# Both MLP products of a transformer block as seven block products instead of eight

## The chip, the core and the metric

The kernel runs on one core of one Trainium2 chip. The core has five engines that run side by side, each with an in-order queue of its own: TensorE (PE, the 128x128 multiplier; PEld is its loading of the stationary operand), VectorE (DVE), ScalarE (ACT), GpSimd (POOL) and SyncE (SP). SP, ACT and POOL also issue transfers, which 16 DMA engines carry out. SBUF is the memory on the chip, PSUM the accumulators of TensorE, DRAM the memory behind the DMA engines. The metric is the time of one execution in microseconds, the median of several.

## The reference, cut to what matters

One layer of a streaming encoder over 512 tokens of width 2048: attention first, then a squared-ReLU MLP of width 8192, both residual, and a final norm.

```
def sq_relu_mlp(h, w1, w2):
    return jnp.square(jax.nn.relu(h @ w1)) @ w2
...
    h = h + stick_breaking_mixer(rms_norm(h, norm_mix), w_qkv, w_o)
    h = h + sq_relu_mlp(rms_norm(h, norm_mlp), w1, w2)     # w1 2048 x 8192, w2 8192 x 2048
    return rms_norm(h, final_norm)                          # 512 x 2048
```

Everything is float32. A product is exact to about float32 by splitting each operand into two float32r parts, hi and lo, and adding three products: hi hi, hi lo, lo hi.

## The kernel before

A *panel* is 512 columns of a weight matrix against all 512 tokens. Its weights come in *pieces* of two contraction tiles (256 rows, 512 KB): `load` issues the transfer into `raw` on SP, `split` makes `whi` (ACT, L142) and `wlo = raw - whi` (DVE, L143), and `run` multiplies. `mm3` (L149) issues the three products of one tile pair on lines 151 to 153, each with its own load of the stationary operand. Pieces go round in six buffers of `wp` (three pieces of two parts) and two of `rp`.

The program runs 12 panels for q, k and v with the attention's steps woven in, four panels of the output projection (`o_panels`; `turn_h` transposes the new residual stream into `hT` on TensorE and splits it), and then the MLP: eight chunks of 1024 hidden columns, each two panels of W1 (16 contraction tiles; `evac_1` makes relu, square and the split of it in SBUF) and four panels of W2 (8 contraction tiles; `evac_2` adds the product, times the token's scale, to the residual tiles `hn`). The last W2 panel is computed token block by token block (`run_held`, accumulators `acch`), its last block in two halves of 256 columns, so that the final norm (`finish`) overlaps. In the MLP the residual stream `hn` (16 tiles) and the activations stay in SBUF.

The order on each engine is that of the code as the tile framework's scheduler placed it when the program was built; each engine then works through its own list and waits on semaphores where another engine's result is missing.

Of the kernel before, what the change touches and what calls it, by code (L numbers as in the profile page):

```python
# [12 lines left out]
PSUM = bass.MemoryType.PSUM  # L13

# [11 lines left out]
FC = 1024            # hidden columns of the MLP held on chip at a time  # L26


class Panel:
    """512 weight columns against all 512 tokens: four accumulators of one PSUM bank."""  # L30

    def __init__(self, srcs, nk, acts, weights_still, evac, held=False):
        self.held = held                    # all its weights are on chip at once
# [8 lines left out]
def trunk_kernel(  # L42
    ctx: ExitStack,
    tc: tile.TileContext,
    x: bass.AP,          # [512, 2048], last token first
    x_t: bass.AP,        # its transpose
    g_mix: bass.AP,      # [128, 16]
    g_mlp: bass.AP,      # [128, 16]
    g_fin: bass.AP,      # [1, 2048]
# [4 lines left out]
    out: bass.AP,        # [512, 2048], last token first  # L54
# [6 lines left out]
    acc_a = ctx.enter_context(tc.tile_pool(name="acc_a", bufs=4, space=PSUM))  # L61

# [6 lines left out]
    # ---- constants  # L69
# [15 lines left out]
    ss_h, ms_h, rstd2 = stat[:, 20:36], stat[:, 36:40], stat[:, 40:44]  # L85
# [4 lines left out]
    def rsqrt(dst, v, t0, t1):  # L90
        """dst = v ** -0.5, with one Newton step after the table's square root."""
# [7 lines left out]
    # ---- weight pieces: raw by DMA, then an exact split into two float32r parts  # L99
# [28 lines left out]
    def split(n):  # L128
        while state["split"] < min(n, len(pieces)):
            i = state["split"]  # L130
            load(i + 1)
            raw = raws.pop(i)
            if pieces[i][0].held:
                parts = [(slot(F32R, "whi"), slot(F32R, "wlo")) for _ in range(G)]
                for j, (hi, lo) in enumerate(parts):
                    nc.scalar.copy(hi, raw[:, j, :])
                    nc.vector.tensor_tensor(out=lo, in0=raw[:, j, :], in1=f(hi), op=ALU.subtract)
            else:
                hi = wp.tile([P, G, W], F32R, name="whi", tag="w")
                lo = wp.tile([P, G, W], F32R, name="wlo", tag="w")  # L140
                for js in halves(i):
                    nc.scalar.copy(hi[:, js, :], raw[:, js, :])  # L142
                    nc.vector.tensor_tensor(  # L143
                        out=lo[:, js, :], in0=raw[:, js, :], in1=f(hi[:, js, :]), op=ALU.subtract)
                parts = [(hi[:, j, :], lo[:, j, :]) for j in range(G)]
            splits[i] = parts
            state["split"] += 1

    def mm3(ps, a, b, start, stop):  # L149
        """ps += a.T @ b for (hi, lo) pairs."""  # L150
        nc.tensor.matmul(ps, lhsT=a[0], rhs=b[0], start=start, stop=False)  # L151
        nc.tensor.matmul(ps, lhsT=a[0], rhs=b[1], start=False, stop=False)  # L152
        nc.tensor.matmul(ps, lhsT=a[1], rhs=b[0], start=False, stop=stop)  # L153
# [6 lines left out]
    def run(p, pool, step=None, steps=1, before_held=False):  # L160
        banks = [pool.tile([P, W], F32, name=f"acc{b}", tag="acc") for b in range(4)]
        ng = p.nk // G
        for g in range(ng):
            i = p.first_piece + g
            ahead(i)
            if before_held and g >= 2:
                ahead(i + 1)
# [19 lines left out]
    def run_held(p, pool, spans):  # L187
        """Token block by token block; spans[b] are the column ranges of its accumulators."""
        split(len(pieces))
        parts = [q for g in range(p.nk // G) for q in splits.pop(p.first_piece + g)]  # L190
        for b in range(4):
            ca = slice(b * P, (b + 1) * P)
            for cs in spans[b]:
                bank = pool.tile([P, W], F32, name="acch", tag="acc")
                for k in range(p.nk):
                    act = p.acts(k)
                    hi, lo = parts[k]
                    mm3(bank[:, 0 : cs.stop - cs.start], (act[0][:, ca], act[1][:, ca]), (hi[:, cs], lo[:, cs]),
                        k == 0, k == p.nk - 1)
                p.evac(b, bank, cs)  # L200

    # ---- the attention's panels
    xT, oT, hT = {}, {}, {}
    qT, kT, vv = {}, {}, {}

    def evac_v(grp):
# [333 lines left out]
```

## Time and profile before

| | |
|---|---|
| median of 3 runs | 2197.77 us (2197.66 to 2198.48) |
| span of the profiled execution, first to last instruction | 2196.5 us |
| TensorE busy | 2184.8 us, 99% |
| VectorE busy | 869.6 us, 40% |
| ScalarE busy | 666.0 us, 30% |
| GpSimd busy | 36.8 us, 2% |
| moved by DMA | 216.53 MB, 99 GB/s |

The page gives the span of the profiled execution, 2196.5 us, 1.3 us below the median of the runs (2197.77), which also holds what lies before the first and behind the last instruction; a time that is summed from the trace is made against the span, and those 1.3 us are added. Matmuls overlap in the array, so their rate is read from the distance between the starts of neighbours, not from the length of one.

### The profile page before, as it was taken

Reading aid. Unit: us, or ns where it says so; the run is one execution under the profiler, and the core shown is the slowest. Engines: PE = TensorE matmul, PEld = TensorE weight load, DVE = VectorE, ACT = ScalarE, POOL = GpSimd, SP = SyncE. Lnnn points to the kernel's source line nnn. Section 1 sums busy time; section 2 is a strip of 40 time slices with the busy share of each in tenths; the row PEclk is TensorE's granted clock in tenths of the full one; section 3 lists DMA queues with packets and bytes.
Section 4 is the critical chain, followed back from the end, with each engine's and each line's share of the span. In section 5 each row is a group of like instructions: output and inputs, shape, how many; then the busy total and the mean of one; then the engine's idle time right before and its main releaser. Section 6 shows DMA issues by size and latency. Waiting matters only on the chain.

```text
span 2196.5 us, 23826 instructions
## 1 busy us (share of the span) xinstructions
PE 2184.8 (99%) x9870; PEld 1812.8 (83%) x9870; DVE 869.6 (40%) x1024; ACT 666.0 (30%) x897; POOL 36.8 (2%) x91
## 2 busy tenths in 40 slices
PE   9999999999999999999999999999999999999998
PEld 7888888888888888888888888888888888888887
DVE  7354453553553333433333333333332433343334
ACT  6343342442442332212212212212211311221234
POOL 0000000000010000000000000000000000000013
PEclk9999999999999999999999999999999999999999
DMA  5222222222234333333233333333323333333323
GB/s 192 96 77 81 92 77 87 85 79 95 79 115 134 106 96 96 96 96 96 97 98 99 100 96 96 96 96 96 96 97 97 99 99 98 96 96 96 96 96 125
DMA packets 129101, 216.53 MB, mean 99 GB/s; under 512 B 8016, under 2 KB 40800, under 8 KB 128864
## 3 DMA queue, kind: packets, MB, share of 16 engines
q1 hardware_dynamic: 125360, 207.66, 30.7%
q10 hardware_dynamic: 3600, 7.34, 1.0%
q8 instruction: 77, 1.26, 0.2%
q14 instruction: 32, 0.26, 0.0%
q0 software_dynamic: 32, 0.01, 0.0%
HBM read 210.78 MB, written 4.19 MB: 98 GB/s over the span
## 4 chain that ended last, share of the span: by engine, by line
PE 98%; DMA 1%; DVE 0%; ACT 0%; issue 0%; SPq 0%; ACTq 0%
PE acc L151 31%; PE acc L153 31%; PE acc L152 31%; PE at L443 1%; DMA raw<-w_qkv_dram 0%; PE z L152 0%; PE ot L152 0%; PE z L153 0%; PE ot L153 0%; PE z L151 0%; PE ot L151 0%; PE acch L153 0%; PE acch L152 0%; PE acch L151 0%; PE at L258 0%; DMA xc<-x_t_dram 0%
## 5 line engine op out<-in xcount | busy, mean ns | idle before, releaser
L143 DVE TENSOR_TENSOR wlo<-raw,whi 128x1024 fp32r<-128x1024 f32 (+1 forms) x381 | 466.8, 1226 | 1080.9 <-ACT whi L142 1077.1
L142 ACT CAST whi<-raw 128x1024 fp32r<-128x1024 f32 (+1 forms) x381 | 400.4, 1051 | 1235.0 <-PE acc L152 1221.0
L151 PE MATMUL acc<-thi,whi 128*128 128x512 f32 x1536 | 599.8, 390 | 0.0
L153 PE MATMUL acc<-thi,wlo 128*128 128x512 f32 x1536 | 598.1, 389 | 0.0
L152 PE MATMUL acc<-tlo,whi 128*128 128x512 f32 x1536 | 597.7, 389 | 0.0
L151 PE MATMUL acc<-whi,ahi 128*128 128x512 f32 x992 | 385.9, 389 | 0.0
L152 PE MATMUL acc<-wlo,ahi 128*128 128x512 f32 x992 | 385.9, 389 | 0.0
L153 PE MATMUL acc<-whi,alo 128*128 128x512 f32 x992 | 385.9, 389 | 0.0
L153 PEld LDWEIGHTS acc<-thi,wlo 128*128 128x128 f32 x1536 | 288.3, 188 | 60.5
L152 PEld LDWEIGHTS acc<-tlo,whi 128*128 128x128 f32 x1536 | 288.4, 188 | 58.9
L151 PEld LDWEIGHTS acc<-thi,whi 128*128 128x128 f32 x1536 | 288.4, 188 | 59.0
L152 PEld LDWEIGHTS acc<-wlo,ahi 128*128 128x128 f32 x992 | 186.2, 188 | 38.7
L153 PEld LDWEIGHTS acc<-whi,alo 128*128 128x128 f32 x992 | 186.2, 188 | 38.7
L151 PEld LDWEIGHTS acc<-whi,ahi 128*128 128x128 f32 x992 | 186.2, 188 | 38.6
L151 PE MATMUL acc<-whi,ohi 128*128 128x512 f32 x256 | 101.2, 395 | 0.0
L152 PE MATMUL acc<-wlo,thi 128*128 128x512 f32 x256 | 100.1, 391 | 0.6 <-DVE wlo L143 0.6
L151 PE MATMUL acc<-whi,thi 128*128 128x512 f32 x256 | 100.3, 397 | 0.5 <-ACT whi L142 0.5
L153 PE MATMUL acc<-whi,olo 128*128 128x512 f32 x256 | 100.0, 390 | 0.0
L153 PE MATMUL acc<-whi,tlo 128*128 128x512 f32 x256 | 99.9, 391 | 0.0
L152 PE MATMUL acc<-wlo,ohi 128*128 128x512 f32 x256 | 99.7, 389 | 0.0
L284 DVE SCALAR_TENSOR_TENSOR h<-acc,stat,h 128x512 f32<-128x512 f32 x112 | 83.2, 749 | 34.1 <-PE acc L153 34.1
L432 DVE TENSOR_TENSOR_SCAN rest<-rest,first 128x512 f32<-128x512 f32 (+1 forms) x64 | 52.5, 820 | 15.6 <-ACT rest L430 15.6
(109 smaller groups left out, 1238.4 us busy)
## 6 DMA issues: line engine op xcount, KB each, us to landing
raw<-w_dram SPq DMA_DIRECT2D x256, 512.0 KB, 3.7
raw<-w_qkv_dram SPq DMA_DIRECT2D x130, 256.0 KB, 3.0
raw<-w_o_dram SPq DMA_DIRECT2D x32, 512.0 KB, 3.6
raw<-w_qkv_dram SPq DMA_DIRECT2D x31, 512.0 KB, 3.8
h<-x_dram ACTq DMA_DIRECT2D x16, 256.0 KB, 4.0
xc<-x_t_dram SPq DMA_DIRECT2D x7, 512.0 KB, 4.9
y_dram<-h SPq DMA_DIRECT2D x8, 256.0 KB, 3.3
y_dram<-h ACTq DMA_DIRECT2D x8, 256.0 KB, 3.4
```

Source lines behind the costliest of these rows:

```text
L142: nc.scalar.copy(hi[:, js, :], raw[:, js, :])
L143: nc.vector.tensor_tensor(out=lo[:, js, :], in0=raw[:, js, :], in1=f(hi[:, js, :]), op=ALU.subtract)
L151: nc.tensor.matmul(ps, lhsT=a[0], rhs=b[0], start=start, stop=False)
L152: nc.tensor.matmul(ps, lhsT=a[0], rhs=b[1], start=False, stop=False)
L153: nc.tensor.matmul(ps, lhsT=a[1], rhs=b[0], start=False, stop=stop)
L284: nc.vector.scalar_tensor_tensor(out=t, in0=ps, scalar=rstd2[:, tb : tb + 1], in1=t, op0=ALU.mult, op1=ALU.add)
L432: nc.vector.tensor_tensor_scan(out=rest[:, 1 : n + 1], data0=rest[:, 1 : n + 1], data1=first[:, 0:n], initial=0.0, op0=ALU.mult, op1=ALU.max)
L443: nc.tensor.transpose(out=ps[:, kb * P : (kb + 1) * P], in_=beta[:, kb * P : (kb + 1) * P], identity=ident)
```

## The change

Each MLP product is computed as C = A B on 2x2 blocks with seven block products (the form of Strassen and Winograd) instead of eight. For W1 a *unit* is 512 hidden columns (16 units): tokens in halves of 256, contraction in halves of 1024, columns in halves of 256. For W2 a unit is 1024 output columns of one chunk of 1024 hidden columns (16 units): tokens in halves of 256, the chunk in halves of 512, columns in halves of 512. The weights are the stationary operand in W1 (so 256 token columns move) and the moving one in W2 (512 columns move).

The sums on the weight side are made by DMA: a chain's tile is loaded with one block (SP), multiplied, and then further blocks are added to it by loads from GpSimd's queue with `accum_op=ALU.add`. Chain a carries four of the seven products (three additions), chain b two (one addition), chain c one. A unit has 3 MB of plain weight loads (6 of 512 KB) and eight accumulating loads of 512 KB. The sums on the token side (`mix_tasks`: seven pairs of hi and lo, L312, L313, L318) are made by ACT and DVE, for W1 once, for W2 for every chunk. The activations between the products are stored to DRAM by ACT (`store`) and fetched again by SP (`mix_a`); the residual stream waits in DRAM during W1. The results of the seven products are combined in PSUM where two share an accumulator (x three to four products, y two), and by ACT and DVE (`evac_1`) or by adding each product into one tile of `hn` with its sign (`evac_2`). One RMS scale known early (`condition`, from half the columns) is multiplied into the stream ahead of W1, and the rest of it behind W2. `side` is a list of small tasks of which `run2` starts one or two behind each half of a product.

```
+    ORDER = (
+        ("11", "a", "x", (0, 1)),
+        ("12", "c", "z", None),
+        ("s1", "a", "y", (1, 1)),
+        ("s4", "b", "y", (0, 1)),
+        ("s2", "a", "x", (1, 0)),
+        ("s3", "b", "x", None),
+        ("22", "a", "x", None),
+    )
...
+    def split2(upto):
...
+            for pc in range(2):
+                raw = u.raw[chain, pc]
+                hi = wp.tile([P, u.jn, u.width], F32R, name="whi", tag="w")
+                lo = wp.tile([P, u.jn, u.width], F32R, name="wlo", tag="w")
+                nc.scalar.copy(hi, raw)
+                nc.vector.tensor_tensor(out=lo, in0=raw, in1=f(hi), op=ALU.subtract)
+                parts.append((hi, lo))
+                if more:
+                    nc.gpsimd.dma_start(raw, u.block(*more, pc), accum_op=ALU.add)
...
+    def run2(ui, still, pools, pace=1, only=range(7)):
...
+            left, _, name, _ = ORDER[p]
+            i = 7 * ui + p
+            split2(i + 2)
+            parts = ready.pop(i)
+            fresh = (name, 0) not in u.acc
+            for s in range(2):
...
+                for j in range(2 * u.jn):
+                    hi, lo = (t[:, j % u.jn, :] for t in parts[j // u.jn])
+                    ah, al = (t[:, j % 2, :] for t in mixed[left][u.key(j)])
+                    start, stop = fresh and j == 0, j == 2 * u.jn - 1
+                    if still:
+                        mm3(ps, (hi[:, cs], lo[:, cs]), (ah, al), start, stop, True)
+                    else:
+                        mm3(ps, (ah[:, cs], al[:, cs]), (hi, lo), start, stop, True)
+                u.evac(p, s, ps)
+                for _ in range(pace):
+                    if side:
...
+    def evac_2(c, q):
+        def go(p, m, ps):
+            th, nh, sign, last = SINK[p]
...
+            nc.vector.scalar_tensor_tensor(out=t, in0=ps, scalar=by, in1=t, op0=ALU.mult, op1=ALU.add)
...
-        for i, p in enumerate(mlp_panels[1:]):
-            pool = acc_a if i % 2 else acc_b
...
+        for c in range(NC2):
+            for q in range(2):
...
+                if c < NC2 - 1:
+                    fetch_a, tasks = mix_a(c + 1, q)
+                    side.extend([fetch_a, None, None, None, *tasks])
```

`split2` is called for the next product at the start of each; a product's weights are two tiles (`pc` 0 and 1), and the six `wp` buffers hold one and a half products.

VectorE in a stretch of W2, first before the change: `wlo` is the low part of a weight piece, `h` a residual tile to which an accumulator is added.

```order
L143 TENSOR_TENSOR wlo<-raw,whi 128x1024 x4
L284 SCALAR_TENSOR_TENSOR h<-acc_9915,stat,h 128x512
L284 SCALAR_TENSOR_TENSOR h<-acc_9916,stat,h 128x512
L284 SCALAR_TENSOR_TENSOR h<-acc_9917,stat,h 128x512
L284 SCALAR_TENSOR_TENSOR h<-acc_9918,stat,h 128x512
L143 TENSOR_TENSOR wlo<-raw,whi 128x1024 x4
```

After the change, in a W2 unit while the fourth product (s4) and the start of the fifth (s2) run: the three `wlo` rows are the two weight tiles of the fifth product and the first of the sixth (s3); `11l`, `12l`, `s1l` and `mix` belong to the next chunk's token-side sums, acc_14284 and acc_14302 are the halves of accumulator y, acc_14200 one of x.

```order
L400 TENSOR_TENSOR wlo<-ra,whi 128x1024
L313 TENSOR_TENSOR 11l<-ain,11h 128x512
L503 SCALAR_TENSOR_TENSOR h<-acc_14284,stat,h 128x512
L313 TENSOR_TENSOR 12l<-ain,12h 128x512
L318 TENSOR_TENSOR mix<-ain 128x512
L400 TENSOR_TENSOR wlo<-ra,whi 128x1024
L503 SCALAR_TENSOR_TENSOR h<-acc_14302,stat,h 128x512
L400 TENSOR_TENSOR wlo<-rb,whi 128x1024
L313 TENSOR_TENSOR s1l<-mix,s1h 128x512
L503 SCALAR_TENSOR_TENSOR h<-acc_14200,stat,h 128x512
L318 TENSOR_TENSOR mix<-mix,ain 128x512
```

Weight parts, residual additions and token-side sums now alternate one by one, so a late one holds up the next weight tile.

VectorE where the MLP begins, before: behind the last output-projection panel come three small operations and one split tile for each weight piece.

```order
L494 RECIPROCAL stat<-stat 128x4
L264 SCALAR_TENSOR_TENSOR tlo<-at,gl,thi 128x512
L143 TENSOR_TENSOR wlo<-raw,whi 128x1024
L264 SCALAR_TENSOR_TENSOR tlo<-at,gl,thi 128x512
L143 TENSOR_TENSOR wlo<-raw,whi 128x1024
```

After, a little later (VectorE has by then finished the last panel's residual tiles and transposed half of them into `hin`); `12l` is needed by the second product of the first unit, the rows up to `22l` belong to one group of contraction tiles, and the last row begins the same list for the next group.

```order
L313 TENSOR_TENSOR 12l<-hin,12h 128x512
L318 TENSOR_TENSOR mix<-hin 128x512
L313 TENSOR_TENSOR s1l<-mix,s1h 128x512
L318 TENSOR_TENSOR mix<-mix,hin 128x512
L318 TENSOR_TENSOR mix<-hin,mix 128x512
L313 TENSOR_TENSOR s4l<-mix,s4h 128x512
L313 TENSOR_TENSOR s2l<-mix,s2h 128x512
L318 TENSOR_TENSOR mix<-hin 128x512
L313 TENSOR_TENSOR s3l<-mix,s3h 128x512
L313 TENSOR_TENSOR 22l<-hin,22h 128x512
L298 TENSOR_TENSOR hin<-ht,gl 128x512 x2
L313 TENSOR_TENSOR 12l<-hin,12h 128x512
```

The `12l` of the last group stands behind all sums of the group before it.

GpSimd's list before, from its set-up to the end: small fills for the attention, and the final gain (`g_bc`, L298).

```order
L81 COPY first<-ident 128x128
L429 MEMSET rest 128x1 x64
L500 TENSOR_SCALAR g_bc<-g_bc 128x2048
L298 TENSOR_TENSOR h<-h,g_bc 128x512 x15
L298 TENSOR_TENSOR h<-h,g_bc 128x256 x2
```

After, around the step from W1 (tiles of 4x256) to W2 (2x512); each row is so many accumulating loads into the tiles of chain a or b:

```order
L403 DMA ra<-w_dram 128x4x256 x6
L403 DMA rb<-w_dram 128x4x256 x2
L403 DMA ra<-w_dram 128x4x256 x2
L403 DMA ra<-w_dram 128x2x512 x4
L403 DMA rb<-w_dram 128x2x512 x2
```

A list that was all but empty during the MLP now issues eight transfers in each unit, 256 in all.

## Rows read from the trace of the kernel before

**Rows 1.** The page: busy time of each engine, share of the span, instructions.

```profile
PE 2184.8 (99%) x9870; PEld 1812.8 (83%) x9870; DVE 869.6 (40%) x1024; ACT 666.0 (30%) x897; POOL 36.8 (2%) x91
```

**Rows 2.** The page: the chain that ended last, by engine and line.

```profile
PE 98%; DMA 1%; DVE 0%; ACT 0%; issue 0%; SPq 0%; ACTq 0%
PE acc L151 31%; PE acc L153 31%; PE acc L152 31%; PE at L443 1%; DMA raw<-w_qkv_dram 0%; PE z L152 0%; PE ot L152 0%; PE z L153 0%; PE ot L153 0%; PE z L151 0%; PE ot L151 0%; PE acch L153 0%; PE acch L152 0%; PE acch L151 0%; PE at L258 0%; DMA xc<-x_t_dram 0%
```

**Rows 3.** Windows in the MLP: us, busy of each engine, granted clock, DMA share, GB/s.

```profile
1000.00:1500.00 500.00, 500.00 (x2208) 414.01 (x2207) 178.43 (x188) 125.31 (x140) 0.00 (x0) 1.00 0.32 97
1500.00:2100.00 600.00, 600.00 (x2649) 496.82 (x2648) 207.74 (x218) 151.76 (x171) 0.00 (x0) 1.00 0.32 97
```

**Rows 4.** TensorE's timeline at the end: start us, length us, instruction.

```profile
2177.71 0.39 PE L151 MATMUL acch<-whi,ahi 128*128 128x512 f32 x1
2177.93 0.39 PE L152 MATMUL acch<-wlo,ahi 128*128 128x512 f32 x1
...
2182.24 0.39 PE L153 MATMUL acch<-whi,alo 128*128 128x512 f32 x1
2182.47 0.28 PE L151 MATMUL acch<-whi,ahi 128*128 128x256 f32 x1
2182.58 0.28 PE L152 MATMUL acch<-wlo,ahi 128*128 128x256 f32 x1
...
2188.10 0.28 PE L153 MATMUL acch<-whi,alo 128*128 128x256 f32 x1
```

**Rows 5.** Groups by line and shape: busy us, mean ns, idle before and its releaser.

```profile
L143 DVE TENSOR_TENSOR wlo<-raw,whi 128x1024 fp32r<-128x1024 f32 x379 | 465.5, 1228 | 1080.9 <-ACT whi L142 1077.1
L284 DVE SCALAR_TENSOR_TENSOR h<-acc,stat,h 128x512 f32<-128x512 f32 x112 | 83.2, 749 | 34.1 <-PE acc L153 34.1
L277 DVE TENSOR_TENSOR alo<-a,ahi 128x512 fp32r<-128x512 f32 x64 | 44.3, 693 | 6.7
L142 ACT CAST whi<-raw 128x1024 fp32r<-128x1024 f32 x379 | 399.2, 1053 | 1234.8 <-PE acc L152 1221.0 <-issue 7.4 <-DMA raw<-w_qkv_dram 3.3
L151 PEld LDWEIGHTS acc<-whi,ahi 128*128 128x128 f32 x992 | 186.2, 188 | 38.6
```

**Rows 6.** VectorE's timeline in W1: starts of neighbours with nothing between them.

```profile
1530.73 1.23 DVE L143 TENSOR_TENSOR wlo<-raw,whi 128x1024 fp32r<-128x1024 f32 x1 [4.21 <-ACT whi L142]
1531.87 0.68 DVE L275 TENSOR_TENSOR a<-r 128x512 f32<-128x512 f32 x1
1532.66 0.69 DVE L277 TENSOR_TENSOR alo<-a,ahi 128x512 fp32r<-128x512 f32 x1
1533.27 0.69 DVE L275 TENSOR_TENSOR a<-r 128x512 f32<-128x512 f32 x1
```

**Rows 7.** Transfers by line: count, KB each, median us from issue to landing.

```profile
raw<-w_dram SPq DMA_DIRECT2D x256, 512.0 KB, 3.7
gm<-g_mix_dram POOLq DMA_DIRECT2D x1, 8.0 KB, 3.5
```

**Rows 8.** GpSimd's timeline: its one transfer, 128 rows of 64 bytes.

```profile
1.22 0.73 POOL L72 DMA_DIRECT2D gm<-g_mix_dram  x1 [0.79 <-POOLq L529]
```

**Rows 9.** A weight buffer comes free, ScalarE and VectorE follow (timeline, W2).

```profile
1502.02 0.39 PE L152 MATMUL acc<-tlo,whi 128*128 128x512 f32 x1
1502.44 1.05 ACT L142 CAST whi<-raw 128x1024 fp32r<-128x1024 f32 x1 [4.38 <-PE acc L152]
1503.53 1.23 DVE L143 TENSOR_TENSOR wlo<-raw,whi 128x1024 fp32r<-128x1024 f32 x1 [4.21 <-ACT whi L142]
```

**Rows 10.** GpSimd's and VectorE's groups at the end: busy us, mean ns, idle before.

```profile
L298 POOL TENSOR_TENSOR h<-h,g_bc 128x512 f32<-128x512 f32 x15 | 21.1, 1426 | 1510.8 <-ACT junk L297 1510.5
L298 POOL TENSOR_TENSOR h<-h,g_bc 128x256 f32<-128x256 f32 x2 | 1.4, 723 | 3.3 <-ACT junk L297 3.3
L293 DVE SCALAR_TENSOR_TENSOR h<-acch,stat,h 128x256 f32<-128x256 f32 x2 | 1.0, 484 | 1.4 <-PE acch L153 1.4
```

More of the change, by code (lines that the diff above doesn't have):

```diff
@@ L61, in trunk_kernel @@
     acc_a = ctx.enter_context(tc.tile_pool(name="acc_a", bufs=4, space=PSUM))
+    dram = ctx.enter_context(tc.tile_pool(name="dram", bufs=1, space=DRAM))
+    h_dram = {(tb, n): dram.tile([P, W], F32, name=f"h_{tb}_{n}") for tb in range(NT) for n in range(4)}
+    a_dram = {(u, th, kh): dram.tile([P, 2, 256], F32, name=f"a_{u}_{th}_{kh}")
+              for u in range(DF // 512) for th in range(2) for kh in range(2)}
     def slot(dt=F32, name="t"):
@@ L132, in split, with mm3 @@
             raw = raws.pop(i)
[L133 to L146, printed above, removed]
+            hi = wp.tile([P, G, W], F32R, name="whi", tag="w")
+            lo = wp.tile([P, G, W], F32R, name="wlo", tag="w")
+            for js in halves(i):
+                nc.scalar.copy(hi[:, js, :], raw[:, js, :])
+                nc.vector.tensor_tensor(
+                    out=lo[:, js, :], in0=raw[:, js, :], in1=f(hi[:, js, :]), op=ALU.subtract)
+            splits[i] = [(hi[:, j, :], lo[:, j, :]) for j in range(G)]
             state["split"] += 1
[L149 to L153, printed above, removed]
+    def mm3(ps, a, b, start, stop, goes_on=False):
+        nc.tensor.matmul(ps, lhsT=a[0], rhs=b[0], start=start, stop=False, skip_group_check=goes_on)
+        nc.tensor.matmul(ps, lhsT=a[0], rhs=b[1], start=False, stop=False, skip_group_check=goes_on)
+        nc.tensor.matmul(ps, lhsT=a[1], rhs=b[0], start=False, stop=stop, skip_group_check=goes_on)
     def ahead(i):
@@ L165, in run @@
             ahead(i)
-            if before_held and g >= 2:
-                ahead(i + 1)
+            if behind and g == ng - 1:
+                behind()
             parts = splits.pop(i)
@@ L185, in run @@
                     p.evac(b, banks[b])
[L187 to L203, printed above, removed]
+    xT, oT = {}, {}
     qT, kT, vv = {}, {}, {}
@@ new lines, in trunk_kernel @@
+    homes = {}
+    units2 = []
+    ready = {}
+    done = {"split": 0}
+    def split2(upto):
+        while done["split"] < min(upto, 7 * len(units2)):
+            i = done["split"]
+            u, (_, chain, _, more) = units2[i // 7], ORDER[i % 7]
+            parts = []
+            for pc in range(2):
+                raw = u.raw[chain, pc]
[6 more added lines that the diff above has]
+                    nc.gpsimd.dma_start(raw, u.block(*more, pc), accum_op=ALU.add)
+            ready[i] = parts
+            done["split"] += 1
+            nxt = units2[i // 7 + 1] if i // 7 + 1 < len(units2) else None
+            if nxt:
+                if i % 7 == 0:
+                    nxt.fetch("a")
+                elif i % 7 == 1:
+                    nxt.fetch("c")
+                elif i % 7 == 5:
+                    nxt.fetch("b")
@@ new lines, in trunk_kernel, with load_h, load_gain @@
+    g_bc = {}
+    def load_h(ns):
+        for n in ns:
+            for tb in range(NT):
+                hn[tb, n] = slot(F32, "h")
+                nc.sync.dma_start(hn[tb, n], h_dram[tb, n])
+    def load_gain():
+        for n in range(4):
+            g_bc[n] = slot(F32, "gain")
+            nc.scalar.dma_start(g_bc[n], g_fin[:, n * W : (n + 1) * W].broadcast_to([P, W]))
+            nc.gpsimd.tensor_scalar(out=g_bc[n], in0=g_bc[n], scalar1=-0.5, scalar2=None, op0=ALU.mult)
+        nc.vector.memset(ss_f, 0.0)
@@ L497, in trunk_kernel @@
[L497 to L507 removed]
+            if n == 2:
+                units2[0].fetch("a")
+                units2[0].fetch("b")
```

299 lines of the change are left out of this document (223 added, 76 removed).

## The prediction

> **What bounds the kernel now.** I read the page from the top: TensorE is busy 99% of the span [rows 1] and the chain that ended last is TensorE for 98% of it, nearly all in the three lines of `mm3` [rows 2]. The windows inside the MLP say the same of that stage alone: TensorE never pauses, at a granted clock of 1.00 of full speed (2.4 GHz), while VectorE works 36%, ScalarE 25%, GpSimd not at all, and the DMA engines are 32% busy at 97 GB/s [rows 3]. So only fewer or faster matmuls help, and what the change loads onto the other engines counts only where TensorE must wait for it.
>
> The rate of a matmul comes from the starts of neighbours at the end of the trace [rows 4]. Of 512 columns: 2177.71 to 2182.24 is 20 distances, 0.2265 us each. Of 256 columns: 2182.47 to 2188.10 is 47 distances, 0.1198 us each. Two narrow ones cost 0.2396, 6% more than one wide one.
>
> **TensorE's sum.** The MLP has two times 3072 wide products; 24 of them are made as 48 narrow ones in the last token block. Removed: 6120 x 0.2265 + 48 x 0.1198 = 1391.9 us. Added for W1: 16 units x 7 products x 2 halves x 8 tiles x 3 = 5376 narrow, 644.0 us. Added for W2: 16 x 7 x 2 x 4 x 3 = 2688 wide, 608.8 us. Together 1252.8, so TensorE has 139.1 us less to do. The transposes of the residual stream stay 64. One product lasts 48 x 0.1198 = 5.75 us in W1 and 24 x 0.2265 = 5.44 us in W2.
>
> **What VectorE and ScalarE get.** In a W1 unit VectorE has 14 low parts of weights at 1.23 us [rows 5] and six half tiles, some 20 us of 40.3; ScalarE 14 high parts at 1.05 us and about 7 us of results. Both keep up. In a W2 unit VectorE has 14 x 1.23, 14 residual additions at 0.75 and, for the next chunk, 11 token-side operations at 0.69 [rows 5]: 35.3 of 38.1 us. Neighbours overlap, though: a low part is followed after 1.14 us instead of 1.23, a small operation after 0.61 instead of 0.69 [rows 6], which makes some 32.5 us. The second weight tile of a product is the tight place. Its buffer comes free when TensorE has finished the first tile of the product before, at three quarters of that product; ScalarE follows 0.2 us behind, VectorE 1.1 us later [rows 9], so the low part is there 4.08 + 0.2 + 1.1 + 1.23 = 6.6 us after the product before began, and TensorE asks for it at 5.44 + 1.36 + 0.23 = 7.0. I walked a W2 unit down VectorE's list (the second listing in the change), each row at the later of its input and the row before. With the full lengths, the low parts of the third, fifth, sixth and seventh product come 0.2, 0.5, 0.55 and 0.6 us late: the small sums stand ahead of them. That is 1.9 us for each of the 14 units that prepare a chunk, 27 us. With the overlapped distances every one is just in time: 0. I take the middle, 13 us. In W1 the same place has 0.3 us to spare without any small sums; in the last W1 unit, which prepares the first chunk at double pace, the walk loses 2 us.
>
> **The start of the MLP.** Here the sums of the last contraction tiles can begin only when the last output panel is finished. In VectorE's list (the fourth listing) the last `12l` stands behind two scalings, four transposed tiles, three weight tiles and ten sums. Walked from the first product's start, it is ready at about 17 to 19 us; TensorE has by then done the first product (5.75) and 16 transposes and has reached the tiles that need it at 9 to 11. With a smaller wait for weights behind it I put 9 us. Before, TensorE had no such wait (the trace's chain has no VectorE share, [rows 2]).
>
> **The end.** The last result is now 512 columns wide: VectorE's addition takes 0.75 instead of 0.48, GpSimd's gain 1.43 instead of 0.72 [rows 10]. I add 1 us.
>
> **The accumulating loads.** The trace has none; this is the open price. What a load may take: between the two uses of a tile lie two products, less 2.3 us for its own split behind it: 11.5 - 2.4 = 9.1 us in W1, 10.9 - 2.4 = 8.5 in W2. A longer load stops TensorE, three times in a unit (chain a), so each us too much costs 48 us in W1 and 48 in W2. From below, the price is a plain load of the same 512 KB, 3.7 us [rows 7]. From above: it reads the weights and the tile that it adds to, so twice a plain load, 7.4, and GpSimd must issue 512 rows in W1 and 256 in W2; its one transfer of 128 rows held it 0.73 us [rows 8], so 2.9 and 1.5 more: 10.3 and 8.9. Nothing below 3.7 can gain, since TensorE doesn't wait for loads now. The middle is 7.0 in W1 and 6.3 in W2. I take these, so that the loads are hidden: 0. At the upper ends the cost is 48 x 1.2 + 48 x 0.4 = 77 us.
>
> The engines' capacity gives a second view. At 32% for 97 GB/s [rows 3] they would be full at 303 GB/s. A unit moves 3.15 MB of plain weights, 1.05 MB of activations and 4.19 MB by accumulation: 8.4 MB, 27.7 us of a 40.3 or 38.1 us unit. If an accumulated byte counts twice, 12.6 MB need 41.5 us, and the units become 1.2 and 3.4 us longer: 74 us, in place of (not beside) the 77.
>
> The Trainium skill, "Collectives: The Full Stack", section "The bandwidth ceiling: the fold count and why AG ≠ RS ≠ AR", says that an added stream needs two source reads on the same ring, which halves its rate. By that rule the 74 us are due and the time would be some 2158. No row here has a transfer that adds, so the rule stands as the second case below.
>
> **Sum.** 2196.5 - 139.1 + 13 + 2 + 9 + 1 = 2082.4 us of span; with the 1.3 us between span and median (2197.77), 2083.7, say **2084**. Its own range is 2062 to 2110: from no wait at all (2059) to the 27 us in W2 and ten more at the loads.
>
> **The rivals.**
> (a) *The loads are nearly hidden*: they take about double, by either view. The time is 2084 + 74 or 77 = 2160; anything from 2110 to 2193 belongs here. For it: the tile must be read as well as the weights, rows of 1 KB in W1, and bursts of plain loads meet them. Against it: the engines are two thirds idle now.
> (b) *The other side: the accumulating loads set the pace.* If one takes three plain loads, 11.1 us, each of chain a's three is 2.0 us late in W1 and 2.6 in W2: 48 x 2.0 + 48 x 2.6 = 221 us, 2305. It decides from 48 (L - 9.1) + 48 (L - 8.5) = 114, that is from L = 10.0 us. For it: software issue, and eight in a unit on one in-order queue, so a late one delays the next. Against it: the only software-issued row landed in 3.5 us [rows 7], and even the upper bound made of rows lies at the edge only.
> (c) *The gain isn't there*: narrow matmuls with a fresh stationary operand each might be slower in a long stream than in 48. If each cost its whole 0.188 us of weight load [rows 5], W1 alone would lose 370 us. Against it: the 48 in a row [rows 4] are exactly one product of W1, at 0.1198 from the first to the last.
>
> **Chances.** Forecast (2062 to 2110) 0.47, (a) 0.21, (b) 0.27 with half of it above 2250, (c) 0.02, within 0.2% by balance 0.03; 0.2% is 4.4 us and about what a measurement of this kernel can tell from no change. Faster is 0.47 + 0.21 = 0.68, the same 0.03, slower 0.29. The range of 8 in 10 reaches from 2062 to 2250, because the unknown load pushes only upwards.
>
> **What would show it.** In the changed kernel's trace: narrow matmuls in W1 at 0.12 us; TensorE's work in the MLP some 1253 us; the issue rows of the accumulating loads at less than 8.5 us to landing (hidden), about 8.5 to 10 (a), or more (b); waits of TensorE for `wlo` and `whi` whose own releaser is such a load; a gap of some 9 us within the first unit; VectorE above 85% busy in W2 with waits of less than 1 us in the units that prepare a chunk and none in the last two. A DMA share near 0.7 in W1 speaks for accumulated bytes that count once, near 1.0 for twice. Wrong would be above all an accumulating load beyond 10 us, or a W2 in which VectorE's list delays residual additions that TensorE needs for its accumulators.

## The result, and the profile after

The changed kernel takes 2110.51 us (median of 4 runs, 2108.42 to 2111.31) against 2197.72 us of the kernel before beside it: the ratio is 0.9602 [0.9588, 0.9615], 87 us less. The forecast was 2084, 26 us too low. Its own range ended at 2110: the measured time lies half a microsecond above it and so, by the letter, in the range that the prediction gave to its rival (a) (2110 to 2193), though (a)'s price of 74 to 77 us for the loads is not what was found (16 us, experiment 1); the range of 8 in 10, 2062 to 2250, holds it. The profiled execution spans 2106.6 us, against 2082.4 in the sum. Of the executions reported below one took 5276.48 us, in experiment 3, for a reason that the record does not show, and the times there are of the others.

The page of the changed kernel: busy time, queues with packets, megabytes and their share of the 16 DMA engines' span, and the chain that ended last (it answers to [rows 1, 2]).

```profile
PE 2060.9 (98%) x11766; PEld 1811.8 (86%) x11766; DVE 1242.2 (59%) x1509; ACT 968.5 (46%) x1328; POOL 354.1 (17%) x349
...
q0 software_dynamic: 102432, 134.24, 40.2%
q1 hardware_dynamic: 144048, 195.07, 28.1%
...
PE 83%; DMA 7%; DVE 4%; issue 3%; ACT 2%; POOL 1%; SPq 0%; ACTq 0%; POOLq 0%; DVEq 0%
```

TensorE was 98% of the chain before and is 83% now, although it is busy for 98% of the span. So the other 17%, some 350 us, is not lost time: the chain also runs through transfers and splits beside which TensorE worked on. It shows which work has come close to holding TensorE up, and transfers head it.

The accumulating loads by tile, KB each and median us from issue to landing (answers to [rows 7]), and windows in W1, at the joint of W1 and W2, and in W2 (columns as in [rows 3]).

```profile
ra<-w_dram POOLq DMA_DIRECT2D x192, 512.0 KB, 7.2
rb<-w_dram POOLq DMA_DIRECT2D x64, 512.0 KB, 7.4
```

```profile
840.00:1400.00 560.00, 559.79 (x4660) 559.10 (x4659) 266.02 (x276) 299.51 (x402) 143.96 (x112) 1.00 1.02 208
1440.00:1520.00 80.00, 66.67 (x321) 55.39 (x320) 54.70 (x70) 36.58 (x49) 11.94 (x10) 0.89 0.91 245
1560.00:1960.00 400.00, 397.80 (x1745) 326.50 (x1744) 345.66 (x414) 192.67 (x225) 101.58 (x85) 1.00 0.96 219
```

The accumulating loads land in 7.2 to 7.4 us over the whole run; by stage the median is 7.9 us in W1 (840 to 1400 us) and 7.0 in W2 (1560 to 1960), where 7.0 and 6.3 were estimated. The DMA share is 1.02 in W1. TensorE still hardly pauses there: 559.79 of 560 us. At the joint it is busy 66.67 of 80 us, at a granted clock of 0.89.

The pitch of the matmuls, on TensorE's timeline (start us, length us): 28 distances of 256 columns, 24 of 512.

```profile
815.03 0.28 PE L149 MATMUL acc<-12l,whi 128*128 128x256 f32 x1
...
818.38 0.28 PE L150 MATMUL acc<-12h,wlo 128*128 128x256 f32 x1
...
1477.71 0.39 PE L148 MATMUL acc<-whi,s4h 128*128 128x512 f32 x1
...
1483.15 0.39 PE L148 MATMUL acc<-whi,s2h 128*128 128x512 f32 x1
```

They are 0.1196 and 0.2267 us, those of [rows 4]. So the work was forecast rightly, and the loss is in waits. From the start of each unit's first `11` matmul the time beyond the pure matmuls can be put to stages (40.25 us for a W1 unit and 38.05 for a W2 unit, the prediction's sums):

```
stage (first matmul to first matmul)        us      matmuls   beyond
first W1 unit       791.97 to  847.30      55.33     40.25     15.1   (1.6 of it the transposes)
W1 units 2 to 15    847.30 to 1412.94     565.64    563.50      2.1
the joint: last W1 unit, first two of W2
                   1412.94 to 1549.88     136.94    116.35     20.6
W2 units 3 to 15   1549.88 to 2053.37     503.49    494.65      8.8
last W2 unit       2053.37 to 2095.09      41.72     38.05      3.7
```

Together 50.3. The kernel before had 4.3 beyond its MLP matmuls in the same stretch (792.00 to 2188.2), 1.4 of it the last matmuls of the output projection. Behind the last matmul stand 11.5 us now (2095.1 to 2106.6) and 8.3 before: 50.3 - 4.3 + 3.2 = 49.2 us lost, where the sum had 25.

### The profile page after: what moved, and what is told of

It reads as the page before. It is cut to its first block, busy times and chain, and to the rows that moved or that the text cites. A ratio compares the mean times of both kernels' runs of the same rounds, so it can differ in the third digit from the quotient of the medians.

```text
span 2106.6 us, 29753 instructions
## 1 busy us (share of the span) xinstructions
PE 2060.9 (98%) x11766; PEld 1811.8 (86%) x11766; DVE 1242.2 (59%) x1509; ACT 968.5 (46%) x1328; POOL 354.1 (17%) x349
## 3 DMA queue, kind: packets, MB, share of 16 engines
q0 software_dynamic: 102432, 134.24, 40.2%
## 4 chain that ended last, share of the span: by engine, by line
PE 83%; DMA 7%; DVE 4%; issue 3%; ACT 2%; POOL 1%; SPq 0%; ACTq 0%; POOLq 0%; DVEq 0%
PE acc L149 26%; PE acc L150 26%; PE acc L148 26%; DMA ra<-w_dram 4%; DMA ain<-a 2%; DVE wlo L400 2%; ACT whi L399 1%; PE at L686 1%; DMA raw<-w_dram 1%; POOL ra L403 0%; PE z L149 0%; PE ot L149 0%; PE z L150 0%; PE ot L150 0%; PE z L148 0%
## 5 line engine op out<-in xcount | busy, mean ns | idle before, releaser
L400 DVE TENSOR_TENSOR wlo<-ra,whi 128x1024 fp32r<-128x1024 f32 x256 | 314.6, 1229 | 232.4 <-ACT whi L399 227.4
L403 POOL DMA_DIRECT2D ra<-w_dram x192 | 239.0, 1245 | 1010.2 <-DVE wlo L400 988.7
L399 ACT CAST whi<-ra 128x1024 fp32r<-128x1024 f32 x256 | 267.8, 1051 | 303.4 <-PE acc L149 235.4
L141 DVE TENSOR_TENSOR wlo<-raw,whi 128x1024 fp32r<-128x1024 f32 (+1 forms) x129 | 156.6, 1215 | 264.1 <-ACT whi L140 263.0
L140 ACT CAST whi<-raw 128x1024 fp32r<-128x1024 f32 (+1 forms) x129 | 134.8, 1045 | 267.8 <-PE acc L149 253.7
L148 PE MATMUL acc<-thi,whi 128*128 128x512 f32 x512 | 201.0, 393 | 0.0
L150 PE MATMUL acc<-thi,wlo 128*128 128x512 f32 x512 | 199.8, 390 | 0.0
L149 PE MATMUL acc<-tlo,whi 128*128 128x512 f32 x512 | 199.4, 389 | 0.0
L150 PEld LDWEIGHTS acc<-thi,wlo 128*128 128x128 f32 x512 | 96.1, 188 | 20.6
L149 PEld LDWEIGHTS acc<-tlo,whi 128*128 128x128 f32 x512 | 96.2, 188 | 19.2
```

Of the source, the lines that this page charges most:

```text
L141: nc.vector.tensor_tensor(out=lo[:, js, :], in0=raw[:, js, :], in1=f(hi[:, js, :]), op=ALU.subtract)
L399: nc.scalar.copy(hi, raw)
L400: nc.vector.tensor_tensor(out=lo, in0=raw, in1=f(hi), op=ALU.subtract)
L403: nc.gpsimd.dma_start(raw, u.block(*more, pc), accum_op=ALU.add)
```

## The experiments

All times are medians. "Units" are lengths from first matmul to first matmul, as in the table. They come from one profiled execution each, and units that two kernels share differ by up to 3 us, so less than that is not read from them.

**1. Plain loads in place of the accumulating ones.**

```
-                    nc.gpsimd.dma_start(raw, u.block(*more, pc), accum_op=ALU.add)
+                    nc.gpsimd.dma_start(raw, u.block(*more, pc))
```

> The accumulating loads become plain loads into the same tiles at the same places, so the weight sums are left out. Theory A (the 26 us beyond the forecast lie at the two joints of the MLP, where sums and fetches are issued late): the products of W1 keep their time, the DMA share between 840 and 1400 us falls from 1.02 to about 0.7, the joint between W1 and W2 loses a little less because its fetches land in 4 us instead of 6 to 7; 2095 to 2108 us. Rival B (the doubled traffic of the accumulating loads is what costs the time): the late weights and fetches go, 2060 to 2085. Rival C (VectorE's list in W2 costs the time): 2108 to 2112, no change.

Measured: 2094.61 us (2092.97 to 2095.51), ratio 0.953 [0.9516, 0.9545]: 16 us faster. Its queue of the same 134.24 MB on the page, its transfers, and its windows:

```profile
q0 software_dynamic: 36896, 134.24, 21.3%
```

```profile
ra<-w_dram POOLq DMA_DIRECT2D x192, 512.0 KB, 4.7
```

```profile
840.00:1400.00 560.00, 560.00 (x4669) 560.00 (x4668) 266.72 (x278) 301.32 (x403) 83.87 (x112) 1.00 0.70 209
1440.00:1520.00 80.00, 74.28 (x370) 62.55 (x369) 65.56 (x84) 42.39 (x56) 9.98 (x15) 0.98 0.79 273
```

The bytes are the same, and the engines' time for them is 21.3% in place of 40.2% of the span: an accumulated byte costs them 1.9 times a plain one. The DMA share in W1 is 0.70 without and 1.02 with accumulation. The W1 units are the same 40.3 us both ways; the joint falls from 137.0 to 125.3. The time is at the lower edge of theory A's 2095 to 2108 and well above B's 2060 to 2085. But the joint falls by 12 us, more than A's "a little less", which speaks for B's cause there. ScalarE and VectorE work through the same lists in the same order in both kernels, so the joint's 12 us are not due to another order. The 3rd to 15th W2 unit still lose 6.2 us, against 8.8.

**2. Every accumulating load twice.** The line above is issued a second time.

> Every accumulating load is issued twice, so a weight block is added twice and the products are of other sums. The slack of the prediction (9.1 us in W1, 8.5 in W2, 48 us for each us beyond in either) gives, for 2 x 7.2 = 14.4 us, 48 x 5.3 + 48 x 5.9 = 538 us more: about 2650. If the engines' time sets the pace (3.3 us of all 16 engines for each of eight more in a unit, 26 us a unit): about 2950. If the loads have more slack than the prediction worked out: under 2250.

Measured: 3022.87 us (3018.39 to 3025.04), ratio 1.3752 [1.3732, 1.3773]; the W1 units become 68 to 72 us. A window in W1:

```profile
840.00:1400.00 560.00, 391.85 (x2684) 372.89 (x2684) 151.81 (x160) 169.90 (x233) 166.10 (x128) 0.84 0.97 180
```

The engines are nearly full (0.97), and a unit grows by 30 us for eight more accumulations, 3.8 us each, near the 3.3 us that each takes of all 16 (40.2% of 2106.6 us over 256 loads); the time is nearest to the 2950 of that case. But GpSimd's queue stands still too: the second load of a tile waits until the first has landed, and all loads behind it wait with it (us in total, times, longest; L404 is the second load).

```profile
POOL ra L404 <- DMA ra<-w_dram: 914.4, 178, 11.8
```

The expectation counted a pair's own time and not what stands behind it in the queue, and the run does not part this from the engines' time. What it shows is that the kernel has no room for a second set of such loads.

**3. The `12` parts first at the start of the MLP.** Of the side tasks in the first product, those of the last two contraction tiles are taken sum by sum, not tile by tile.

```
-                            else:
+                            elif n < 3:
                                 turns.extend(mixes[kp - 4][1:])
+                    if n == 3:
+                        for i in range(1, 7):
+                            turns.extend(mixes[kp][i] for kp in (2, 3))
```

> At the start of the MLP the two '12' low parts of the last contraction tiles are put ahead of their ten other sums. Theory A: TensorE's 11.7 us wait at the second product falls to about 3 us and the clock stays at its upper level, so 2100 to 2103 us. Rival: the ten sums are only moved, and the third to fifth product wait for them instead; 2108 to 2112.

Measured: 2107.78 us (2106.29 to 2111.22), ratio 0.9593 [0.9579, 0.9608]: 2.7 us, within the two intervals. TensorE's waits on its timeline, first in the changed kernel, then in this one:

```profile
811.30 0.58 PE L148 MATMUL acc<-12h,whi 128*128 128x256 f32 x1 [11.67 <-DVE hin L298]
811.68 0.41 PE L149 MATMUL acc<-12l,whi 128*128 128x256 f32 x1
811.89 0.41 PE L150 MATMUL acc<-12h,wlo 128*128 128x256 f32 x1
```

```profile
802.58 0.39 PE L148 MATMUL acc<-12h,whi 128*128 128x256 f32 x1 [2.03 <-DVE hin L301]
816.87 0.38 PE L148 MATMUL acc<-s2h,whi 128*128 128x256 f32 x1 [1.02 <-ACT whi L402]
818.46 0.38 PE L150 MATMUL acc<-s2h,wlo 128*128 128x256 f32 x1 [0.85 <-DVE wlo L403]
822.13 0.39 PE L148 MATMUL acc<-s2h,whi 128*128 128x256 f32 x1 [1.02 <-ACT whi L402]
823.39 0.39 PE L150 MATMUL acc<-s2h,wlo 128*128 128x256 f32 x1 [0.52 <-DVE wlo L403]
827.88 0.38 PE L148 MATMUL acc<-s4h,whi 128*128 128x256 f32 x1 [1.85 <-ACT y L473]
```

The wait falls by 9.6 us, but 5.3 us of new waits follow in the next products, where the splits of the weights now stand behind the sums. The first unit is 52.4 us in place of 55.3. A variant with the sums spread over the first four products:

```
-        run2(0, True, {"x": acc_a}, pace=len(side), only=range(1))
+        run2(0, True, {"x": acc_a}, pace=5, only=range(1))
```

> As early_12, but of the ten sums behind the two '12' five are made half a product later and the rest in the second to fourth product. The early order won 9 us at the second product and gave some 5 back in the third to fifth, where low parts of weights stood behind the sums: if so, the first unit falls from 52.4 us (55.3 before) to about 48, the run to some 2103 us. If the sums are needed as early as they were made: 52 us or more, 2107 to 2110.

Measured: 2105.9 us (median of three, 2103.89 to 2110.02), ratio 0.9584 [0.9568, 0.96], and a first unit of 50.3 us. The unit gains 5 us, not the 7 expected, and the median 4.6, at the edge of the intervals.

**4. Other orders at the joint.** First, fetches of activations put ahead on SP's queue:

```
-                for pl in range(2):
-                    fetch_a, tasks = mix_a(0, pl)
-                    side.extend([fetch_a, *tasks])
+                got = [mix_a(0, pl) for pl in range(2)]
+                side.extend([fetch_a for fetch_a, _ in got])
+                for _, tasks in got:
+                    side.extend(tasks)
...
-                if c == 0 and q == 0:
-                    side.append(lambda: load_h((2, 3)))
...
-                    side.extend([fetch_a, None, None, None, *tasks])
+                    h23 = (lambda: load_h((2, 3))) if c == 0 and q == 0 else None
+                    side.extend([fetch_a, h23, None, None, *tasks])
```

> The activations of a chunk are fetched ahead of the other transfers on SP's queue at the joint of W1 and W2: both fetches of the first chunk ahead of the weights of chain b, the fetch of the next chunk ahead of the second eight residual tiles. Theory A: the waits of 7.2, 1.5, 1.9 and 1.9 us and the low clock behind the longest go, 2096 to 2101 us. Rival B (the DMA engines are full there, so whatever stands ahead, something else is late): 2106 to 2112.

Measured: 2115.62 us (2110.45 to 2117.28), ratio 0.9623 [0.9607, 0.9639]: no gain, 5 us more. The joint has 139.8 us in place of 137.0. TensorE's waits in it:

```profile
1447.50 0.58 PE L148 MATMUL acc<-s3h,whi 128*128 128x256 f32 x1 [4.20 <-ACT u L475]
...
1493.85 0.76 PE L148 MATMUL acc<-whi,s3h 128*128 128x512 f32 x1 [2.13 <-DVE h L503]
```

The 7.17 us wait that it aimed at became 2.13, and others took its place. Second, the sums 5.4 us later:

```
-                    side.extend([fetch_a, None, None, None, *tasks])
+                    side.extend([fetch_a, None, None, None, None, None, *tasks])
```

> In W2 the sums of a chunk are made two half products (5.4 us) later after their fetch; nothing else changes. If ScalarE and VectorE stand still because a fetch is late: less waiting in the first W2 unit (48.1 us) and in the others, 2098 to 2104 us. If VectorE is simply full: no change, 2108 to 2112. If later sums collide with the next chunk's first product: slower, 2112 to 2118.

Measured: 2111.36 us (2109.93 to 2114.42), ratio 0.961 [0.9594, 0.9626], no change; the first two W2 units have 90.4 us where the changed kernel has 90.5. So neither of the two other orders that were tried helped at the joint; theory A is not borne out there, and an order that helps is not ruled out.

**5. No reload of the residual at the joint.** The 16 loads (4.2 MB) are left out.

```
-                nc.sync.dma_start(hn[tb, n], h_dram[tb, n])
...
+            if c == 0 and p in (0, 2, 3, 6):
+                nc.vector.tensor_scalar(out=t, in0=ps, scalar1=by, scalar2=None, op0=ALU.mult)
```

> The residual tiles are not loaded back at the joint of W1 and W2 (16 loads, 4.2 MB): the first addition into each tile writes only the scaled product, so the residual is left out of the output. Theory D (the DMA engines, full at 1.02 in W1, get the residual and three fetches on top there, so everything is late): the last W1 unit and the first two W2 units, 137.0 us now, 116.5 without any wait, fall to about 125, the run to some 2098 us. Rival E (only the order on SP's queue and the waits for single fetches count): they stay above 133, 2107 or more.

Measured: 2098.49 us (2096.67 to 2099.62), ratio 0.9547 [0.9532, 0.9561]: 12 us, theory D's number. The window at the joint:

```profile
1440.00:1520.00 80.00, 77.63 (x392) 66.55 (x392) 66.11 (x84) 43.80 (x58) 18.46 (x16) 0.98 0.97 230
```

TensorE is busy 77.63 of 80 us, 11 more than in the changed kernel. In this kernel and those built on it the unit borders inside the joint are blurred, so the last W1 unit and the first four of W2 are taken together: 200.6 us, against 213.8 in the changed kernel. Without the 16 loads SP's queue is shorter too, so this run alone does not part the bytes from the order (rival E). Experiment 1 does: there every load keeps its place, only the engines' time for the accumulation goes, and the joint gives back 12 us all the same.

**6. No sums on the token side after the first chunk.**

```
-                    side.extend([fetch_a, None, None, None, *tasks])
+                    side.extend([fetch_a])
...
-        x.key = lambda j: (c, j // 2)
+        x.key = lambda j: (0, j // 2)
```

> The sums on the token side for the chunks 2 to 8 are left out and the first chunk's operands are used in all of W2; all fetches stay. Rival C (VectorE's list is what costs W2 its time) and the tasks' waits for late fetches together: the first two W2 units fall from 90.5 to about 83, the units 3 to 14 of W2 from 8.3 us of waiting to under 3, 2095 to 2100 us. Theory D (late weights, whoever waits): the waits for accumulating loads stay, 2104 to 2110.

Measured: 2121.78 us (2121.32 to 2122.66), ratio 0.9654 [0.964, 0.9668]: slower, which neither theory had. Nothing reads the fetched tiles now, so nothing holds the fetches back, and those of several chunks run at once. The first three W2 units grow to 45.8, 46.4 and 56.3 us. From then on ten of the next eleven units take 38.1 us, without a wait, although every accumulating load is still there. The fetches of several chunks at once would crowd out the weights (D's mechanism, made worse by accident); that is the likely reading and was not tested by itself. The run does not say whether it is the sums or their wait for a fetch that costs time in W2; experiments 1 and 8 bear on that.

**7. A version that acts on the cause.** The residual comes back one tile a unit from the third W2 unit on, and VectorE adds it:

```
+                    if c:
+                        at = 2 * (c - 1) + q
+                        load, add = residual(at % 4, at // 4)
+                        side.extend([fetch_a, load, None, None, *tasks, add])
```

> The residual comes back one tile a unit, from the third W2 unit on (the last four in the 15th), into a spare slot, and VectorE adds it there; the joint has no reload. Theory D (4.2 MB on top of full engines at the joint): the joint gives back what no_reload gave, some 13 us, and a tile a unit (0.26 MB, 0.9 us of all engines, and 0.7 us of VectorE) costs up to 0.4 us each in 12 units; 2096 to 2103 us. Rival: the engines have no room for a tile anywhere in W2, so the 13 us are given back there; 2107 to 2112.

Measured: 2104.83 us (2100.07 to 2107.69), ratio 0.9574 [0.9561, 0.9587]: 6 us faster, between theory D's 2096 to 2103 and the rival's 2107 to 2112. The last W1 unit and the first four of W2 give back 14.6 us (199.2). The 5th to 16th W2 unit take 478.8 in place of 468.5, so 10 of it is paid there (up to 0.4 in each of 12 units was expected), 3 of them in the unit of the next edit. Both had a part of the truth: the joint gives its time back, and W2 has little room for the tiles. The factor -0.5 of the gain moved into the row factor:

```
-            nc.gpsimd.tensor_scalar(out=g_bc[n], in0=g_bc[n], scalar1=-0.5, scalar2=None, op0=ALU.mult)
...
-        nc.vector.tensor_scalar(out=v, in0=last, scalar1=1.0 / D, scalar2=base, op0=ALU.mult, op1=ALU.add)
+        nc.vector.tensor_scalar(out=v, in0=last, scalar1=-0.5 / D, scalar2=tmp[:, tb : tb + 1], op0=ALU.mult, op1=ALU.add)
```

> The factor of -0.5 moves from the gain tiles (four GpSimd operations that wait for the gain's load, with accumulating loads queued behind them) into the row factor at the end. If those four delay the accumulating loads of the 14th W2 unit (40.6 us, 2.5 over its matmuls): that unit falls to about 38.5 us and the run to some 2108 us. If the unit is late for another reason: 2109 to 2112, no change that can be told.

Measured: 2106.1 us (2104.67 to 2108.38), ratio 0.9584 [0.9571, 0.9597]; the 14th W2 unit has 38.8 us, against 40.6 in the changed kernel and 41.2 to 43.8 in the six kernels of experiments 3, 4, 5 and 7 that keep the scaling there. In experiment 6 GpSimd does the same four operations 400 us earlier, at 1575 to 1582 us, and the unit has 38.1; with plain loads (experiment 1) it has 38.4. So the scaling costs that unit its time where accumulating loads stand behind it; the gain in the median, 4 us, is at the edge of the intervals. All three edits:

> late_residual, early_12_spread and no_gain_scaling together. If the three causes are apart: 13 less some 4 at the joint, 3 to 5 at the start, 2 at the gain; 2090 to 2096 us. If what one gives another takes back (the DMA engines stay full): 2098 or more.

Measured: 2093.09 us (2089.46 to 2096.85), ratio 0.9523 [0.9509, 0.9537], 17 us faster than the changed kernel and the best of this study that does the whole computation. The first unit has 50.3 us.

**8. All three with plain loads.** The weight sums are left out, as in experiment 1.

> all_three with plain loads in place of the accumulating ones, so the weight sums are left out. It shows how much of what is still lost in all_three (5 us in the last W1 unit, some 15 in the 5th to 16th W2 unit) comes from the engines' traffic. If the late fetches of W2 are late because the engines are full: the 5th to 16th W2 unit, 475 us in all_three, fall to about 465 and the run to 2080 to 2085. If they are late by their order and by the wait for a free slot alone: 473 or more there, 2088 to 2094.

Measured: 2080.56 us (2079.16 to 2081.9), ratio 0.9466 [0.945, 0.9482]. The 5th to 16th W2 unit fall from 475 to 461 us. W2 in a window:

```profile
1560.00:1960.00 400.00, 399.49 (x1763) 330.46 (x1762) 352.39 (x427) 194.10 (x224) 58.99 (x83) 1.00 0.69 231
```

VectorE is busy 352.39 of 400 us, 88%, more than in the changed kernel (345.66, above), and TensorE 399.49. So a VectorE that is 88% busy need not hold TensorE up, and in this list the 14 us were the engines' traffic. The list is not that of the changed kernel, though: with the residual's additions in it the scheduler placed the sums otherwise. The changed kernel's own list with plain loads is experiment 1, and its 5th to 16th W2 unit take 466 us there, against 468.5.

## Why the prediction was right, and where 26 us stayed

**Right: the sum of the matmuls.** Seven products for eight took off 139 us at the pitches of [rows 4], now measured in 815 to 818 and 1478 to 1483 us. Rival (c) is out.

**Right: the accumulating load's length and its limit.** 7.9 us to landing in W1 and 7.0 in W2 against 7.0 and 6.3. The limits of 9.1 us in W1 and 8.5 in W2 can be read where single loads passed them. Two of them stand in the chain (start us, us, what); a third was issued at 1841.76 us, and the split of its tile on ScalarE could start at 1851.41, when it had landed (9.57 us). TensorE's waits behind the three follow.

```profile
1234.98 9.72 DMA ra<-w_dram
...
1460.96 8.95 DMA ra<-w_dram
```

```profile
1841.76 1.20 POOL L403 DMA_DIRECT2D ra<-w_dram  x1 [2.59 <-DVE wlo L400]
...
1851.41 2.00 ACT L399 CAST whi<-ra 128x1024 fp32r<-128x1024 f32 x2 [1.97 <-DMA ra<-w_dram]
```

```profile
1247.14 0.39 PE L150 MATMUL acc<-22h,wlo 128*128 128x256 f32 x1 [0.18 <-DVE wlo L400]
...
1472.37 0.50 PE L149 MATMUL acc<-wlo,s1h 128*128 128x512 f32 x1 [0.29 <-DVE wlo L400]
...
1853.78 0.50 PE L149 MATMUL acc<-wlo,22h 128*128 128x512 f32 x1 [0.75 <-DVE wlo L400]
```

By the limits they are 0.6, 0.5 and 1.1 us late; TensorE's products there are 0.43, 0.58 and 1.08 us longer than 5.76 and 5.44. Rival (b) needed a usual load of 10 us, and the usual one has 7.9 at most.

**Right, but not as it was weighed: the bytes count about twice.** The prediction's mark for that was a DMA share near 1.0 in W1: it is 1.02, and 0.70 with plain loads (0.69 was worked out: 27.7 of 40.3 us). The Trainium skill, "Collectives: The Full Stack", section "The bandwidth ceiling: the fold count and why AG ≠ RS ≠ AR", says of reduce-scatter that its add needs two source reads on one ring and so runs at half the rate; this trace, of a local load, has nearly the same ratio (40.2% against 21.3% for the same bytes). The 74 us that the capacity view made of it did not follow: W1 units 2 to 15 lost 2.1 us in all, not 1.2 each. In the steady units of this kernel a share of 1.0 was thus the edge and not a loss; the loss came where something more was put on top. The whole price of the accumulation is the 16 us of experiment 1.

**Wrong: "the loads are hidden: 0", at the joint.** This is the step that failed, and the largest part of the 26 us. The sum had 2 us for the last W1 unit and some 0.9 for each of the first two W2 units (13 us over 14); they lost 20.6. The prediction held the accumulating loads against a steady unit and did not add what the joint moves besides: 4.2 MB of residual, and two fetches of activations (2.1 MB) in a W1 unit that has none otherwise. The engines have no room left there: their share is 1.10 just before TensorE's longest stop (first row of the windows below). With the same lists and loads that cost the engines less, 12 us of the 21 go (experiment 1); without the residual's 4.2 MB, 13 us (experiment 5); the two other orders of experiment 4 return nothing. How a late transfer becomes a stop of TensorE is to be seen on the timelines of SP, ScalarE, VectorE and TensorE in the changed kernel:

```profile
1454.87 9.67 SPq L529 DMA_DIRECT2D h<-h  x8
1466.32 9.59 SPq L529 DMA_DIRECT2D h<-h  x8
1475.96 7.09 SPq L348 DMA_DIRECT2D ain<-a  x4
```

```profile
1493.17 0.62 ACT L312 CAST 11h<-ain 128x512 fp32r<-128x512 f32 x1 [5.56 <-DMA ain<-a]
```

```profile
1493.82 0.69 DVE L313 TENSOR_TENSOR 11l<-ain,11h 128x512 fp32r<-128x512 f32 x1 [4.95 <-ACT 11h L312]
1494.43 0.75 DVE L503 SCALAR_TENSOR_TENSOR h<-acc,stat,h 128x512 f32<-128x512 f32 x1
```

```profile
1487.76 0.39 PE L150 MATMUL acc<-whi,s2l 128*128 128x512 f32 x1
1495.32 0.76 PE L148 MATMUL acc<-whi,s3h 128*128 128x512 f32 x1 [7.17 <-DVE h L503]
1495.88 0.63 PE L149 MATMUL acc<-wlo,s3h 128*128 128x512 f32 x1
1496.31 0.63 PE L150 MATMUL acc<-whi,s3l 128*128 128x512 f32 x1
```

```profile
1470.00:1487.00 17.00, 16.27 (x71) 12.82 (x70) 9.34 (x10) 5.59 (x6) 6.23 (x6) 1.00 1.10 291
1495.00:1499.00 4.00, 3.32 (x7) 2.15 (x7) 1.56 (x4) 1.57 (x2) 0.00 (x0) 0.50 0.79 236
```

ScalarE waits 5.56 us for a fetched tile that TensorE needs only two units later. VectorE waits for ScalarE with the `11l` of that tile, and behind it in its list stands the residual addition that reads the accumulator with which TensorE has to go on. TensorE stops for 7.17 us for work that is not urgent, and then starts matmuls every 0.43 us (1495.88, 1496.31) in place of 0.2265: the granted clock was 1.00 of 2.4 GHz in front of the pause and is 0.50, so 1.2 GHz, behind it. The prediction had named this as a sign of being wrong ("a W2 in which VectorE's list delays residual additions that TensorE needs for its accumulators") and had no price for it; nor had it one for matmuls at the lower clock behind a wait.

**Near by luck, wrong in its reason: 13 us of VectorE's order in W2.** VectorE is 86% busy there, as forecast, and the units of W2 do wait, 8.8 us in the 3rd to 15th. The walk with the full lengths put the waits at the third, fifth, sixth and seventh product of a unit. Experiment 1 has the same list, and between 1549 and 1950 us none of these products waits for it. So the walk with overlapped distances, which gave 0, was right. The 8.8 us come from two other things. Accumulating loads that land late make waits at the fifth and seventh product (the third example above is one), and they are gone in experiment 1. Late fetches make waits at the first product, and these stay there: five, 2.7 us together, at a DMA share of 0.65, with 6.2 us lost in these units. One of them on ScalarE and TensorE in experiment 1, and the same place on ScalarE in experiment 8:

```profile
1691.24 0.62 ACT L312 CAST 11h<-ain 128x512 fp32r<-128x512 f32 x1 [4.06 <-DMA ain<-a]
...
1692.50 1.04 ACT L399 CAST whi<-ra 128x1024 fp32r<-128x1024 f32 x1
```

```profile
1694.85 0.50 PE L149 MATMUL acc<-wlo,11h 128*128 128x512 f32 x1 [0.77 <-DVE wlo L400]
```

```profile
1680.94 1.05 ACT L402 CAST whi<-ra 128x1024 fp32r<-128x1024 f32 x1 [3.02 <-PE acc L149]
1681.89 0.62 ACT L315 CAST 11h<-ain 128x512 fp32r<-128x512 f32 x1
```

In the changed kernel's list the split of the next weights stands behind the sum on a fetched tile, so a late fetch holds up the weights. In experiment 8 the split stands ahead of it, and the product does not wait. So much of the 8.8 us is left when the engines have room (the 2.6 us that go are less than units vary by), and where a wait of TensorE can be followed then, it belongs to the order on ScalarE. That another order alone would return it was not tried.

**Under-sized, and at another instruction: the start.** 9 us forecast, 13.5 measured (15.1 less the transposes): one wait of 11.67 us, and lower-clock matmuls behind it (granted clock 0.58 from 811 to 815 us), which start every 0.21 us (811.68, 811.89) in place of 0.12. The prediction let TensorE stop at the tiles that need the last `12l`. It stops at the first matmul of the product already, and for `hin`, VectorE's read-out of the last transposed tiles: in the code that product's accumulators (`acc_b`) come from the PSUM that the transposes' pool (`att_ps`) gives back. VectorE's place in its list is the one that was named, behind the ten sums of the tile before; the read-out ends some 19 us after the first product began, where 17 to 19 was walked for `12l`. Experiment 3 shows why reordering returns 3 to 5 us and not 11: the sums move in front of the next products' weights.

**Under-sized: the end.** 1 us forecast; 3.2 behind the last matmul and 3.7 within the last unit, which is 41.1 to 41.7 us long in every version but that of experiment 2. No experiment touched it.

**Left open.** The last W1 unit lost 3 to 8 us in every version but that of experiment 2, 3.3 even in experiment 8, with 1.9 us of it a wait of TensorE for `u`, whose copy stands behind the first chunk's sums on ScalarE. Which of these sums it is was not tried.

## What to carry to other kernels

A load that is hidden in the steady state takes the engines' slack with it, so the bill comes where the program changes stage and moves something more: add up the transfers at each joint by engine time, not only in a unit. Where the engines were full here, two other orders only moved the wait; fewer bytes in that stretch helped, and the same bytes spread over the units behind it helped in part. And work for later on an in-order engine should not stand ahead of what TensorE needs next: its late input stops everything behind it.

## What the runs showed of the hardware that was not expected

An accumulating load of 512 KB moves in smaller packets: 102432 for the 134.24 MB, against 36896 for the same bytes loaded plainly. Its issue holds GpSimd for 1.245 us on average, 0.732 for a plain one; these are the groups of the two kernels (busy us, mean ns).

```profile
L403 POOL DMA_DIRECT2D ra<-w_dram x192 | 239.0, 1245 | 1010.2 <-DVE wlo L400 988.7
```

```profile
L403 POOL DMA_DIRECT2D ra<-w_dram x192 | 140.5, 732 | 1088.6 <-DVE wlo L400 1072.2 <-DVE h L503 12.1 <-DMA raw<-w_dram 2.9
```

The number of rows (512 of 1 KB in W1, 256 of 2 KB in W2), from which the prediction worked out 2.9 and 1.5 us of issue, hardly shows in it, as two rows of the chain say, the first from W1 and the second from W2:

```profile
1223.94 1.25 POOL ra L403
...
1908.58 1.17 POOL ra L403
```
